# A 32-byte tile ahead of the weight pools at the right-hand end of SBUF

## The chip, the cores and the metric

The kernel runs on one core of one Trainium2 chip. The metric is the device time of one execution in microseconds, as the median of several runs. A core has five engines that the profile names: PE (TensorE, matmuls; its weight loads stand apart as PEld), DVE (VectorE), ACT (ScalarE), POOL (GpSimd) and SP (SyncE, which here issues most of the transfers). Matmuls read both operands from SBUF, the on-chip memory of 128 partitions, and write to PSUM.

## The reference

One decoder layer (DEPTH = 1) on 256 positions of width 2048, all in float32:

```python
h = rmsnorm(x, g_pre_mix)
proj = h @ w_in                      # 2048 x 15376, split into the inputs of three branches and their gates
oa = gated_head_norm(gated_deltanet(...), az, gn_a)
ob = gated_head_norm(hgrn2(...), bz, gn_b)
oc = memory_attention(cq, rmsnorm(mem, g_mem), w_kv_mem)
merged = ga * (oa @ w_br_a) + gb * (ob @ w_br_b) + gc * (oc @ w_br_c)
x = x + rmsnorm(merged @ w_out, g_post_mix)
h2 = rmsnorm(x, g_pre_mlp)
m = square(relu(h2 @ w_mlp_in)) @ w_mlp_out      # 2048 -> 8192 -> 2048
x = x + rmsnorm(m, g_post_mlp)
```

## The kernel before

Nearly all the time is matrix products of 256 positions with streamed weights. To keep float32 accuracy in the faster format fp32r, each operand is held as two parts, a high part (the value rounded to fp32r) and a low part (the rest), and each product is made as three: high by high, high by low, low by high. Activations are split once; weights are split as they arrive.

**How weights travel.** SP loads a piece of 128 partitions x 2 x 512 float32 (512 KB, 4096 bytes a partition) into a tile `w` (`load_w_raw`, line 193). `split_w` (line 203) lets ACT cast it into `wh` and DVE subtract `wh` from it into `wl`. `w`, `wh` and `wl` have four buffers each in the pool `wp` (line 84), which is placed from the right-hand end of SBUF. All other pools grow from the left.

**Which operand moves.** A matmul holds one operand (stationary, 128 columns wide, loaded by a weight load) and streams the other (moving, up to 512 columns).

- `unit` (line 216) keeps the activation stationary and moves the weights: for each of 16 or 8 rows of blocks and each half of the positions, three matmuls of 512 columns, in the order high activation with `wh`, high with `wl`, low with `wh`.
- `unit_joined` and `unit_stacked`, through `products_joined` (line 248), keep the weights stationary and move the activation's high and low part side by side: one wide matmul of 512 columns with `wh`, and one narrow one of 256 with `wl`. They make a pass of wide ones over some groups, then a pass of narrow ones, and turn the order round for the next groups.

**The stages.** First the memory's keys and values, the projections of the three branches, their inner work (which is spread between the products by generators), the gates, the three branch outputs and `w_out`; this takes `wp` throughout. The MLP follows. `first_weights` (line 1368) loads its first two groups into tiles of the general pool `gp` on the left. Then the MLP has buffers of its own:

```python
pairs = [pair_at(wx, i) for i in range(2)]            # oh0, ol0, oh1, ol1 in pool wx, on the left
raws = [at(wx, "raw0", F32)]
...
weights.close()                                       # in wide_ring: wp is given back
wy = ctx.enter_context(tc.tile_pool(name="wy", bufs=1, side="right", reuse_waits="tile"))
raws.extend(at(wy, f"raw{i}", F32) for i in range(1, 5))
raws.append(g4("raw5", (P, KG, 512)))                 # in gp, on the left
pairs.extend(pair_at(wy, i) for i in range(2, 6))
```

`wide_ring` itself uses pairs 0 and 1; after it, `operand` hands out the six pairs in turn, beginning with pair 0, and `raw` the six landing tiles. For each e of 8, `mlp_in(e)` makes 1024 columns of the hidden layer (for e = 0 the first half with `unit`, else with `unit_stacked`, `oh` and `ol` stationary, the activation `h2h` moving), and `mlp_out(e - 1)` multiplies the 1024 hidden columns of the round before with `w_mlp_out`. There `oh` and `ol` move, and the hidden activations `mh`, `ml` and their sums `sh`, `sl` are stationary. One half of the output is made with seven products in place of eight (`seven`), for which DVE also adds weight tiles. `mlp_out(e)` takes 14 such products of six matmuls each and 8 groups of `unit` with 12 matmuls each: 22 uses of a pair, 180 matmuls.

**Addresses.** Each tile of `wp`, `wy` and `wx` has 4096 bytes a partition. In this program the right-hand end is at byte 229344, which is 32 more than a multiple of 64. So the tiles of `wp` and `wy` all start 32 bytes past a multiple of 64 (96 past a multiple of 128): `w` from 180192, `wh` from 196576, `wl` from 212960, and later `raw1` to `raw4` and pairs 2 to 5 over the same bytes. On the left, `h2h` and `hh` (activations), the general pool, `wx` and the other tiles that the large products read start at multiples of 128. The left-hand pools end at 179392 at most, 800 bytes below.

The order of the instructions on each engine is set by the program and the scheduler, with waits where a buffer has to be free or filled.

Of the kernel before, what the change touches and what calls it, by code (L numbers as in the profile page):

```python
# [10 lines left out]
F32 = mybir.dt.float32  # L11
# [6 lines left out]
P = 128  # L18
# [22 lines left out]
def tile_trunk(ctx: ExitStack, tc, a):  # L41
# [38 lines left out]
    mixing = ctx.enter_context(ExitStack())  # L80
    mk = mixing.enter_context(tc.tile_pool(name="mk", bufs=1))
    lp = mixing.enter_context(tc.tile_pool(name="lp", bufs=1))
    weights = ctx.enter_context(ExitStack())
    wp = weights.enter_context(tc.tile_pool(name="wp", bufs=4, side="right"))

# [1600 lines left out]
```

## Time and profile before

| | us |
|---|---|
| median of 3 runs | 1809.43 (1809.19 to 1810.25) |
| the profiled execution | 1810.36 |
| its span, first to last instruction | 1808.6 |
| PE busy in it | 1796.2 |
| DVE busy | 1303.3 |
| ACT busy | 961.0 |
| granted TensorE clock, mean | 0.999 of full speed |

The profiled execution's time is 1.8 us above its span: that is what lies before the first and after the last instruction. A busy PE is not a PE at its peak, since a matmul's modelled duration overlaps the next one's. What one costs in a dense stream is the distance between two starts, which a window cut at two starts shows.

### The profile page before, as it was taken

The numbers are of one execution on the slowest core, as the hardware profiler recorded it, in microseconds if no ns is written. First come the engines' busy times: TensorE is split into PE (matmuls) and PEld (weight loads), VectorE is DVE, ScalarE is ACT, GpSimd is POOL, SyncE is SP. The second block draws the span as 40 slices with busy tenths as digits, with TensorE's granted clock in tenths as the row PEclk, the third lists the DMA queues.
The fourth block names the chain that finished last, engine by engine and source line by source line (L and its number), as shares of the span: only waits on it lengthen the run. The fifth ranks groups of instructions, "written<-read, shape, count | busy, mean of one in ns | idle before, by whom it ended". The sixth has DMA issues, their size and how long they took to land.

```text
span 1808.6 us, 23962 instructions
## 1 busy us (share of the span) xinstructions
PE 1796.2 (99%) x9053; PEld 1498.4 (83%) x9053; DVE 1303.3 (72%) x1764; ACT 961.0 (53%) x1217; POOL 57.9 (3%) x100
## 2 busy tenths in 40 slices
PE   9999999999999999999999999999999999999998
PEld 7888888888888888888888888888888888888886
DVE  5764768684758487797555556796979797969695
ACT  6644665454555475565444445665545454646453
POOL 0000000400030000000000000000000000000000
PEclk9999999999999999999999999999999999999999
DMA  8565545865587455555666665767767676767683
GB/s 267 203 190 163 171 155 164 221 204 155 157 211 201 137 185 161 150 177 166 179 182 186 228 214 188 236 229 233 230 224 242 218 250 205 256 202 249 205 293 138
DMA packets 188804, 362.84 MB, mean 201 GB/s; under 512 B 14456, under 2 KB 16272, under 8 KB 188304
## 3 DMA queue, kind: packets, MB, share of 16 engines
q1 hardware_dynamic: 181856, 351.32, 61.6%
q0 software_dynamic: 2304, 5.44, 1.6%
q10 hardware_dynamic: 4528, 4.54, 0.9%
q8 instruction: 71, 1.16, 0.3%
q14 instruction: 45, 0.37, 0.1%
HBM read 356.86 MB, written 4.39 MB: 200 GB/s over the span
## 4 chain that ended last, share of the span: by engine, by line
PE 82%; DVE 2%; issue 1%; DMA 0%; ACT 0%; DVEq 0%; POOLq 0%; POOL 0%
PE mm L56 78%; PE pa L56 1%; DVE ol L56 1%; PE kk L56 0%; DMA raw<-in_w_mlp_out 0%; PE bo L56 0%; PE o L56 0%; DVE relu L56 0%; PE pw L56 0%; PE pzt L56 0%; PE tr L56 0%; PE y L56 0%; PE mgT L56 0%; PE oT L56 0%; DVE raw L56 0%
## 5 line engine op out<-in xcount | busy, mean ns | idle before, releaser
L56 DVE TENSOR_TENSOR wl<-w,wh 128x1024 fp32r<-128x1024 f32 (+1 forms) x362 | 436.9, 1216 | 255.5 <-ACT wh L56 230.6
L56 ACT CAST wh<-w 128x1024 fp32r<-128x1024 f32 (+1 forms) x362 | 374.4, 1045 | 376.3 <-PE mm L56 327.1
L56 ACT CAST oh<-raw 128x1024 fp32r<-128x1024 f32 x288 | 299.6, 1051 | 285.6 <-PE mm L56 221.1
L56 DVE TENSOR_TENSOR ol<-raw,oh 128x1024 fp32r<-128x1024 f32 x288 | 342.7, 1218 | 104.4 <-ACT oh L56 70.3
L56 PE MATMUL mm<-wh,hh 128*128 128x512 f32 x1152 | 373.0, 398 | 0.0
L56 PEld LDWEIGHTS mm<-wh,hh 128*128 128x128 f32 x1152 | 216.1, 188 | 51.1
L56 PE MATMUL mm<-h2h,oh 128*128 128x512 f32 x960 | 228.9, 394 | 0.0
L56 PE MATMUL mm<-wl,hh 128*128 128x512 f32 x576 | 227.3, 395 | 0.0
L56 PEld LDWEIGHTS mm<-h2h,oh 128*128 128x128 f32 x960 | 178.5, 188 | 39.8
L56 PE MATMUL mm<-hh,wh 128*128 128x512 f32 x768 | 189.3, 397 | 0.8 <-ACT z L56 0.7
L56 PEld LDWEIGHTS mm<-hh,wh 128*128 128x128 f32 x768 | 141.0, 188 | 32.1 <-ACT z L56 0.9
L56 PE MATMUL mm<-ol,mh 128*128 128x512 f32 x372 | 146.8, 395 | 0.2
L56 PE MATMUL mm<-oh,mh 128*128 128x512 f32 x372 | 146.2, 393 | 0.0
L56 PE MATMUL mm<-oh,ml 128*128 128x512 f32 x372 | 146.1, 395 | 0.0
L56 PEld LDWEIGHTS mm<-wl,hh 128*128 128x128 f32 x576 | 108.2, 188 | 24.5
L56 PEld LDWEIGHTS mm<-h2h,ol 128*128 128x128 f32 x960 | 117.8, 189 | 3.2 <-DVE ol L56 0.6
L56 PE MATMUL mm<-h2h,ol 128*128 128x256 f32 x960 | 119.0, 281 | 0.4 <-DVE ol L56 0.4
L56 PEld LDWEIGHTS mm<-hh,wl 128*128 128x128 f32 x768 | 97.8, 188 | 4.0
L56 PE MATMUL mm<-hh,wl 128*128 128x256 f32 x768 | 100.5, 281 | 0.0
L56 PEld LDWEIGHTS mm<-ol,mh 128*128 128x128 f32 x372 | 69.8, 188 | 17.8 <-DVE ol L56 1.4
L56 PEld LDWEIGHTS mm<-oh,mh 128*128 128x128 f32 x372 | 69.9, 188 | 17.5 <-DVE acc L56 1.1
L56 PEld LDWEIGHTS mm<-oh,ml 128*128 128x128 f32 x372 | 69.9, 188 | 15.9
(363 smaller groups left out, 2217.0 us busy)
## 6 DMA issues: line engine op xcount, KB each, us to landing
w<-in_w_in SPq DMA_DIRECT2D x240, 512.0 KB, 4.1
raw<-in_w_mlp_out SPq DMA_DIRECT2D x170, 512.0 KB, 4.7
raw<-in_w_mlp_in SPq DMA_DIRECT2D x118, 512.0 KB, 4.8
w<-in_w_out SPq DMA_DIRECT2D x32, 512.0 KB, 4.3
w<-in_w_kv_mem SPq DMA_DIRECT2D x30, 512.0 KB, 4.9
w<-in_w_br_c SPq DMA_DIRECT2D x16, 512.0 KB, 3.7
w<-in_w_br_a SPq DMA_DIRECT2D x16, 512.0 KB, 4.5
w<-in_w_br_b SPq DMA_DIRECT2D x16, 512.0 KB, 3.6
```

The source lines that it names most:

```text
L56: ins = op(*args, **kwargs)
```

## The change

A pool `edge` is opened on the right ahead of `wp`, and one tile of 8 float32 a partition (32 bytes) is taken from it. Nothing writes or reads the tile. The pool stays open to the end, so `wp` and later `wy` lie 32 bytes lower: their tiles start at multiples of 64 bytes (64 past a multiple of 128), `w` from 180160, `wh` from 196544, `wl` from 212928.

```diff
     mixing = ctx.enter_context(ExitStack())
     mk = mixing.enter_context(tc.tile_pool(name="mk", bufs=1))
     lp = mixing.enter_context(tc.tile_pool(name="lp", bufs=1))
+    edge = ctx.enter_context(tc.tile_pool(name="edge", bufs=1, side="right"))
+    edge.tile([P, 8], F32, tag="edge", name="edge")
     weights = ctx.enter_context(ExitStack())
     wp = weights.enter_context(tc.tile_pool(name="wp", bufs=4, side="right"))
```

## The prediction

> **What bounds the kernel now.** I read the page first, parts 1, 2, 4 and 5.
>
> ```profile
> span 1808.6 us, 23962 instructions
> PE 1796.2 (99%) x9053; PEld 1498.4 (83%) x9053; DVE 1303.3 (72%) x1764; ACT 961.0 (53%) x1217; POOL 57.9 (3%) x100
> PEclk9999999999999999999999999999999999999999
> PE 82%; DVE 2%; issue 1%; DMA 0%; ACT 0%; DVEq 0%; POOLq 0%; POOL 0%
> L56 DVE TENSOR_TENSOR wl<-w,wh 128x1024 fp32r<-128x1024 f32 (+1 forms) x362 | 436.9, 1216 | 255.5 <-ACT wh L56 230.6
> L56 ACT CAST wh<-w 128x1024 fp32r<-128x1024 f32 (+1 forms) x362 | 374.4, 1045 | 376.3 <-PE mm L56 327.1
> L56 ACT CAST oh<-raw 128x1024 fp32r<-128x1024 f32 x288 | 299.6, 1051 | 285.6 <-PE mm L56 221.1
> L56 DVE TENSOR_TENSOR ol<-raw,oh 128x1024 fp32r<-128x1024 f32 x288 | 342.7, 1218 | 104.4 <-ACT oh L56 70.3
> ```
>
> TensorE streams nearly the whole time. ACT's casts wait for TensorE to give buffers back (327.1 and 221.1 us), not the other way. A change that adds no instruction and no wait can pay only by making matmuls shorter. In the groups "wh,hh" means moving `wh`, stationary `hh`. The mean of 390 to 400 ns is a modelled latency; matmuls overlap, so I read the distance from start to start.
>
> The kernel holds its own comparison. The six operand pairs `oh`, `ol` of the MLP are used in turn: pairs 0 and 1 lie on the left, at multiples of 64 bytes; pairs 2 to 5 on the right, 32 bytes past one. Counting uses after `wide_ring` from 0, use k takes pair k mod 6. `mlp_in(0)` uses 6, each later `mlp_in` 16, each `mlp_out` 22. The last group of `mlp_out(0)` is use 43, pair 1; the second group of the first `unit` in `mlp_out(1)` is use 65, pair 5. Both have 12 matmuls of 512 columns; windows cut at their first starts give their times. (The count in brackets takes in neighbours that reach into a window.)
>
> ```profile
> core 0: us, PE busy (x), PEclk, DMA share, GB/s
> 499.95:508.35 8.40, 8.40 (x37) 1.00 0.75 207
> ...
> 1228.33:1231.09 2.76, 2.76 (x14) 1.00 0.94 298
> 1231.09:1233.81 2.72, 2.72 (x14) 1.00 0.32 118
> 1287.09:1289.89 2.80, 2.80 (x14) 1.00 0.70 203
> 1132.01:1135.66 3.65, 3.65 (x18) 1.00 1.01 348
> 1135.66:1139.41 3.75, 3.75 (x18) 1.00 1.04 379
> 1150.57:1152.49 1.92, 1.92 (x18) 1.00 0.66 172
> 1152.49:1154.36 1.87, 1.87 (x18) 1.00 0.54 148
> 1133.85:1135.66 1.81, 1.81 (x9) 1.00 0.90 306
> 1151.53:1152.49 0.96, 0.96 (x11) 1.00 0.83 254
> ```
>
> With the moving operand at a multiple of 64 (pair 1) a matmul takes 2.72/12 = 226.7 ns; 32 bytes off (pair 5) it takes 2.80/12 = 233.3 ns. Pair 0, just after pair 5, takes 2.76/12 = 230.0: it starts at the slow pace and changes over. The attention branch earlier, all of whose `wh` and `wl` lie on the right, shows the slow pace too: 8.40 us for 36, 233.3 ns.
>
> In `mlp_in` the pairs are stationary and `h2h`, on the left, moves. Sixteen wide matmuls take 3.65 us on pairs 0 and 1, 3.75 on 2 and 3; pair 1 alone, eight of them, 1.81. So 3.75/16 = 234.4 ns becomes 226.3, 8.1 less. The narrow ones (256 columns) go the other way: 0.96/8 = 120.0 ns on pair 1, 1.87/16 = 116.9 on 2 and 3. One wide and one narrow together gain 5.0.
>
> Other tiles and stages agree:
>
> ```profile
> 1107.70 0.61 PE L56 MATMUL mm<-wh,h2h 128*128 128x512 f32 x2
> 1108.15 0.39 PE L56 MATMUL mm<-wl,h2h 128*128 128x512 f32 x1
> 1108.38 0.62 PE L56 MATMUL mm<-wh,h2h 128*128 128x512 f32 x2
> ...
> 1287.09 0.39 PE L56 MATMUL mm<-oh,mh 128*128 128x512 f32 x1
> 1287.32 0.39 PE L56 MATMUL mm<-ol,mh 128*128 128x512 f32 x1
> ...
> 1289.89 0.40 PE L56 MATMUL mm<-oh,sh 128*128 128x512 f32 x1
> ```
>
> The first three rows are from `first_weights`, whose `wh` and `wl` lie on the left in another pool: three starts in 0.68 us, 226.7 ns again.
>
> **The change part by part.** `edge` is never written or read, so it adds no instruction, DMA or wait. It takes 32 bytes, and the 800 free between left and right cover it. `wp` and `wy` move down by 32 together, so which tiles overlap, and so who waits for whom, stays. What moves is the start of `w`, `wh`, `wl`, `raw1` to `raw4` and pairs 2 to 5, and I expect the pace of pair 1 for all of them.
>
> Moving operands on the right. This row counts the matmuls that read `wh`; of these and of as many slots of `wl`, the counts below take the moving ones.
>
> ```profile
> 0.00:1122.60 1122.60, 853.83 (x2880) 1.00 0.62 186
> ...
> L56 PE MATMUL mm<-hh,wh 128*128 128x512 f32 x768 | 189.3, 397 | 0.8 <-ACT z L56 0.7
> L56 PE MATMUL mm<-memT,wh 128*128 128x512 f32 x128 | 31.7, 399 | 0.0
> L56 PE MATMUL mm<-oh,mh 128*128 128x512 f32 x372 | 146.2, 393 | 0.0
> L56 PE MATMUL mm<-oh,sh 128*128 128x512 f32 x112 | 44.6, 398 | 0.0
> L56 PE MATMUL mm<-h2h,oh 128*128 128x512 f32 x960 | 228.9, 394 | 0.0
> ```
>
> - 2880 less the 768 + 128 where `wh` is stationary leaves 1984 with `wh` moving; each product uses `wh` twice and `wl` once, so 992 more: 2976. (24 of them, of `first_weights`, lie on the left; 0.2 us.)
> - In the MLP three products of (372 + 112) each, 1452, of which 4 pairs in 6 are on the right: 968.
> - 3944 x 6.67 ns = 26.3 us.
>
> Stationary operands on the right: 896 pairs of a wide and a narrow matmul, and 4/6 of 960 = 640. 1536 x 5.0 ns = 7.7 us.
>
> The change-over after pair 5 goes: 242 moving uses of pair 0 at (2.76 - 2.72)/12 = 3.3 ns, 0.8 us, and 160 wide ones at (1.84 - 1.81)/8 = 3.8 ns, 0.6 us (1.84 is pair 0's part of the 3.65). Together 35.4 us.
>
> The other engines. The casts `wh<-w`, all on the right, take 1045 ns, those of `oh`, a third on the left, 1051; the subtractions 1216 and 1218. I count nothing for a start there; a per cent of ACT's or DVE's time lies under TensorE except at one place. Transfers into left and right can't be told apart either: the two tables of `raw`, a third of it on the left, land as `w` does.
>
> ```profile
> w<-in_w_in SPq DMA_DIRECT2D x240, 512.0 KB, 4.1
> raw<-in_w_mlp_out SPq DMA_DIRECT2D x170, 512.0 KB, 4.7
> raw<-in_w_mlp_in SPq DMA_DIRECT2D x118, 512.0 KB, 4.8
> ...
> 1278.72:1320.73 42.01, 42.01 (x181) 33.60 (x180) 40.81 (x46) 26.14 (x27) 0.00 (x0) 1.00 0.76 251
> 1365.60:1407.80 42.20, 42.15 (x182) 33.57 (x181) 41.05 (x46) 26.04 (x28) 0.00 (x0) 1.00 0.72 239
> 1539.90:1581.80 41.90, 41.90 (x181) 33.72 (x180) 41.06 (x45) 25.96 (x27) 0.00 (x0) 1.00 0.77 254
> ```
>
> What is late next is in the last three rows, `mlp_out` of three rounds (PE, weight loads, DVE, ACT, POOL). 180 matmuls at 226.7 ns would be 40.8 us, and DVE is busy 40.8 to 41.1 us there. DVE enters such a stretch up to five pairs ahead, since in `mlp_in` it has slack, so I expect it to give back about 0.3 us in each of seven stretches, 2.0 us; the ends are 0 and all that `mlp_out` gains, 968 x 6.67 ns + 0.8 = 7.3 us.
>
> 35.4 - 2.0 = 33.4 us off. The profiled execution took 1810.36 us (its span 1808.6 and 1.8 around it), 0.9 more than the median of the runs, 1809.43. Taken off the median: **1776 us**.
>
> [...]
>
> **The rivals.**
>
> 1. *The start isn't the cause, or 64 isn't the step.* Every pair that is slow lies at the right-hand end, every fast one at a multiple of 128 on the left; after the change the right-hand tiles are 64 past a multiple of 128. So the cause could be the place, or a step of 128, and nothing moves: 1809.4 us. Against: the extra is 6.7 ns, and a column costs (226.3 - 120.0)/256 = 0.415 ns, so it is 16 columns, 64 bytes, one piece of 64 more to fetch. One more piece of 128 would be 13.3 ns. And a stationary operand on the right slows the wide matmul, but quickens the narrow one, which a slow place wouldn't. For: no wide operand 64 past a multiple of 128 is in this trace. Chance 0.12.
> 2. *DVE becomes the bound of `mlp_out`* and takes all 7.3 us there: 1809.4 - 35.4 + 7.3 = 1781 us. For: 41 of 42 us busy. Against: the slack in `mlp_in` and six pairs. It lies in the forecast's range; chance 0.10.
> 3. *Slower: TensorE's granted clock gives.* A stream denser by 3% (6.7 of 233.3 ns) could be answered with a lower clock. Each 0.01 of clock costs some 17.8 us of 1776; the gain is gone at a clock of 0.981, and at 0.97 the time is 1831. Against: the windows on pair 1 and of `first_weights`' stage have 1.00, and the page has 9 in every slice. For: no fast stretch in the trace is longer than a few us. Chance 0.03. [...]
>
> **How the numbers follow.** The forecast, with rival 2 inside, holds 0.85. Its own range: 1771 with nothing given back and 3 us more from stalls that shrink with the pace; 1788 if the stationary side gains nothing (7.7 and 0.6 us) and DVE takes half of `mlp_out`'s 7.3 instead of 2.0 (1.7 more), with 2 us for rounding of the windows. Rival 1 holds 0.12, rival 3 0.03. The range given, 1771 to 1790, leaves these out. Faster by over 0.2%, which is about what a measurement of this kernel can tell from no change: 0.85; within it 0.11; slower 0.04, as a change with no effect can still measure off by that much.
>
> **What would show it.** In the trace after: 12 matmuls of `wh` and `wl` in 2.72 us at any place before 1100 us, not 2.80; wide matmuls with stationary `wh` 226 ns apart and narrow ones 120, not 117; casts and subtractions at 1045 to 1051 and 1216 to 1218 ns still; seven `mlp_out` stretches of 41 to 41.3 us with DVE nearly full; the clock at 1.00. Starts still 233 ns apart in the attention branch would make the prediction wrong by rival 1; DVE as the releaser of TensorE by over 1 us a stretch, by rival 2.

## The result and the profile after

| | before | after |
|---|---|---|
| median, us | 1809.84 (1809.19 to 1810.67) | 1793.23 (1792.62 to 1794.40) |
| ratio, with its 95% interval | | 0.9909 (0.9892 to 0.9926) |
| the profiled execution, us | 1810.36 | 1793.10 |

The changed kernel is faster by 16.6 us, half of the 33.4 that were forecast, and its time lies above the range. The page of after, first the span, then the engines, the clock and the four groups of casts and subtractions:

```profile
span 1791.4 us, 23962 instructions
...
PE 1777.5 (99%) x9053; PEld 1493.9 (83%) x9053; DVE 1303.3 (73%) x1764; ACT 960.6 (54%) x1217; POOL 57.8 (3%) x100
...
PEclk9999999999999999999999999999999999999999
...
L56 DVE TENSOR_TENSOR wl<-w,wh 128x1024 fp32r<-128x1024 f32 (+1 forms) x362 | 437.0, 1217 | 245.7 <-ACT wh L56 223.5
L56 ACT CAST wh<-w 128x1024 fp32r<-128x1024 f32 (+1 forms) x362 | 374.6, 1046 | 365.5 <-PE mm L56 296.0
L56 ACT CAST oh<-raw 128x1024 fp32r<-128x1024 f32 x288 | 299.0, 1051 | 283.0 <-PE mm L56 213.0
L56 DVE TENSOR_TENSOR ol<-raw,oh 128x1024 fp32r<-128x1024 f32 x288 | 343.4, 1221 | 100.8 <-ACT oh L56 68.0
```

The instructions are the same in number, the casts and subtractions take what they took (1046 and 1051, 1217 and 1221 ns), and the clock stays in its top tenth (0.999 on the mean, as before). PE's busy time fell by 18.7 us. So the kind of effect is the one forecast: matmuls got shorter. By how much, windows cut at matmul starts show. First three of before: 36 moving matmuls on stationary `hh` (with `wh` and `wl` moving), 15 wide ones with `wh` stationary, and a stretch of 64 wide and 64 narrow ones with `wh` and `wl` stationary. Columns are as in the prediction's windows:

```profile
683.99:692.39 8.40, 8.40 (x38) 1.00 0.29 71
189.26:192.78 3.52, 3.52 (x17) 1.00 0.85 264
637.79:660.40 22.61, 22.61 (x131) 1.00 0.66 203
```

The same three kinds after the change (the last is the same stretch of the program), then 36 moving on stationary `och` (the output of the memory attention) and another 48 on it, 12 moving of pair 3 (on the right), 12 of pair 1 (on the left), and 16 wide ones with pairs 2 and 3 stationary:

```profile
678.99:687.23 8.24, 8.24 (x38) 1.00 0.53 144
540.09:543.58 3.49, 3.49 (x16) 1.00 0.57 172
630.91:653.24 22.33, 22.33 (x132) 1.00 0.68 208
...
493.69:502.08 8.39, 8.39 (x37) 1.00 0.65 176
376.47:387.46 10.99, 10.99 (x49) 1.00 0.72 166
...
1185.33:1188.08 2.75, 2.75 (x14) 1.00 0.45 130
1215.78:1218.50 2.72, 2.72 (x14) 1.00 0.42 160
1139.72:1143.46 3.74, 3.74 (x19) 1.00 0.68 188
```

On `hh` a moving matmul takes 8.24/36 = 228.9 ns. That is 4.4 less than the 233.3 of before, and not the 226.7 of pair 1 (2.72/12), which still is the pace on the left. Pair 3 agrees: 2.75/12 = 229.2. The gain isn't even: the first `och` stretch still goes at 233.1. That isn't a matter of `och`, since the other goes at 10.99/48 = 229.0, and the 12 matmuls on `hh` just ahead of the slow one take 2.80 us, 233.5 each; what sets the pace there is open. On the stationary side the wide matmuls got almost nothing: 3.74/16 = 233.8 ns against 234.4 for pairs 2 and 3, where 226.3 was expected. With `wh` and `wl` the sum of wide and narrow fell all the same, by 0.28 us for 64 pairs, 4.4 ns a pair of the 5.0 expected: here the narrow ones became shorter, where they were to become longer.

Where the time went, by stage. The first row is before, the second after: the stretch from the first instruction to the same matmul of `first_weights` in the program (5666 matmuls in each).

```profile
0.00:1120.98 1120.98, 1117.75 (x5666) 930.79 (x5667) 751.90 (x1181) 599.48 (x792) 56.78 (x98) 1.00 0.62 185
```

```profile
0.00:1106.34 1106.34, 1102.57 (x5666) 927.54 (x5667) 751.40 (x1181) 599.60 (x792) 56.72 (x98) 1.00 0.62 188
```

Of the profiled executions' 17.3 us, 14.6 came from here, where 24.3 were expected (2976 x 6.67 and 896 x 5.0 ns). The MLP gave only 2.6 us. Its first six `mlp_out` stretches hardly moved: 251.9 us together, 252.6 before. Two of them after, the second being the longest, with PE, weight loads, DVE, ACT and POOL:

```profile
1263.30:1305.30 42.00, 41.81 (x181) 33.55 (x180) 41.04 (x46) 25.91 (x27) 0.00 (x0) 1.00 0.75 250
1436.20:1479.30 43.10, 42.39 (x182) 33.44 (x181) 41.65 (x46) 25.95 (x27) 0.00 (x0) 1.00 0.70 235
```

PE is idle for 0.19 us of the one and 0.71 of the other, where the rows of before have 0.05 at most. Its table of waits (engine, what it waited for, us in total, times, longest) names DVE:

```profile
PE mm L56 <- DVE ol L56: 1.5, 4, 0.6
```

### The profile page after: what moved, and what is told of

Same layout as the page of the kernel before. It is cut to its first block, busy times and chain, and to the rows that moved or that the text cites. A ratio compares the mean times of both kernels' runs of the same rounds, so it can differ in the third digit from the quotient of the medians.

```text
span 1791.4 us, 23962 instructions
## 1 busy us (share of the span) xinstructions
PE 1777.5 (99%) x9053; PEld 1493.9 (83%) x9053; DVE 1303.3 (73%) x1764; ACT 960.6 (54%) x1217; POOL 57.8 (3%) x100
## 4 chain that ended last, share of the span: by engine, by line
PE 82%; DVE 2%; issue 1%; ACT 0%; DMA 0%; DVEq 0%; POOLq 0%; POOL 0%
PE mm L56 77%; DVE ol L56 1%; PE pa L56 1%; PE kk L56 0%; DVE relu L56 0%; PE bo L56 0%; PE o L56 0%; DMA raw<-in_w_mlp_out 0%; PE pzt L56 0%; PE pw L56 0%; PE tr L56 0%; DVE raw L56 0%; DVE ml L56 0%; PE y L56 0%; PE mgT L56 0%
## 5 line engine op out<-in xcount | busy, mean ns | idle before, releaser
L56 DVE TENSOR_TENSOR wl<-w,wh 128x1024 fp32r<-128x1024 f32 (+1 forms) x362 | 437.0, 1217 | 245.7 <-ACT wh L56 223.5
L56 ACT CAST wh<-w 128x1024 fp32r<-128x1024 f32 (+1 forms) x362 | 374.6, 1046 | 365.5 <-PE mm L56 296.0
L56 ACT CAST oh<-raw 128x1024 fp32r<-128x1024 f32 x288 | 299.0, 1051 | 283.0 <-PE mm L56 213.0
L56 DVE TENSOR_TENSOR ol<-raw,oh 128x1024 fp32r<-128x1024 f32 x288 | 343.4, 1221 | 100.8 <-ACT oh L56 68.0
L56 PE MATMUL mm<-wh,hh 128*128 128x512 f32 x1152 | 369.2, 395 | 0.0
```

Of the source, the lines that this page charges most:

```text
L56: ins = op(*args, **kwargs)
```

## The experiments

Three theories of the pace stood at the start. **A**: what counts is the moving or stationary tile's own start, at a multiple of 128 bytes instead of 64. **B**: what counts is the distance between the starts of the two operands, taken round a circle whose length was to be found. **C**: the right-hand end itself is slow in some measure. The left-hand operands of the large products start 128 past a multiple of 256. "Distance" below is the start of the moving operand less that of the stationary one, modulo 256. Where the right-hand tile moves, it was 96 before and is 64 after; where it is stationary, 160 and 192. The edits are shown against the changed kernel, and the times in this section are medians with the ratio to before.

**1. The right-hand tiles at multiples of 128 (distance 0).**

```diff
-    edge.tile([P, 8], F32, tag="edge", name="edge")
+    edge.tile([P, 24], F32, tag="edge", name="edge")
```

> The tile at the right-hand end has 96 bytes instead of 32, so the right-hand tiles start at multiples of 128, as the left-hand ones do. Theory A (the step is 128: a moving or stationary start off a multiple of 128 costs, 6.7 ns at 96 past and 2.3 at 64 past): every pair runs at pair 1's pace, 226.7 ns for a moving matmul, 226.5 and 120 ns for wide and narrow with a stationary one on the right, and the time is 1774 to 1780 us. Theory B (what counts is the distance of the two operands' starts within 128 bytes): the same, 1774 to 1780. Theory C (the right-hand end itself is slower, and 64 is the step): nothing more than the 32-byte tile gives, 1793, moving matmuls at 229 ns. If DVE then holds mlp_out up, its seven stretches stay at 41.5 to 42 us and the time is nearer 1781.

1781.44 us, ratio 0.9843 (0.9828 to 0.9857). Windows of 36 on `och`, 36 on `hh`, 15 wide and 15 narrow with `wh` and `wl` stationary, 12 on pair 2:

```profile
491.68:499.84 8.16, 8.16 (x37) 1.00 0.63 167
678.01:686.17 8.16, 8.16 (x38) 1.00 0.66 193
537.46:540.86 3.40, 3.40 (x17) 1.00 0.55 156
297.62:299.42 1.80, 1.80 (x17) 1.00 0.57 122
1175.59:1178.31 2.72, 2.72 (x14) 1.00 0.71 209
```

Every class now has the pace of pair 1: 226.7 ns moving (8.16/36, 2.72/12) and stationary (3.40/15), 120.0 narrow. That is what the forecast had expected of 32 bytes. C falls: the right-hand end is not slow. A and B both fit.

**2. 64 bytes (distance 32).** The tile of `edge` is `[P, 16]`. 

> The tile has 64 bytes: the right-hand tiles start 32 past a multiple of 128. A (step of 128, absolute): slower than at 128; between 64 past (1793) and 96 past (1809.8) or beyond, since the start is off 64 too. B (distance): 32 instead of 96 apart; a value of its own, the same as 1809.8 if only the size of the distance round the circle counts. C (step of 64): as before, 1809.8, moving matmuls at 233.3 ns.

1808.58 us, ratio 0.9989 (0.9980 to 0.9999). 36 on `hh`, and 15 wide:

```profile
667.19:675.59 8.40, 8.40 (x37) 1.00 0.82 249
544.35:547.85 3.50, 3.50 (x17) 1.00 0.58 171
```

Hardly anything is gained, 1.9 us: 233.3 ns for both kinds (8.40/36, 3.50/15), with the tiles 32 past a multiple of 128 as at 96 past.

**3. No `edge`; the left-hand tiles moved by 96 instead**, by a tile ahead of the first constant on the left. Both sides then start 96 past a multiple of 128, for each by itself a worse start under A, but at distance 0.

```diff
-    edge = ctx.enter_context(tc.tile_pool(name="edge", bufs=1, side="right"))
-    edge.tile([P, 8], F32, tag="edge", name="edge")
...
+    const("lpad", [P, 24])
```

> The kernel before with no tile on the right, but an unused tile of 96 bytes ahead of all others on the left: both sides start 96 past a multiple of 128. A (absolute starts): nothing gets faster, and pairs 0 and 1 become slow as well, 233.3 ns and more for every moving matmul; 1810 to 1825 us. B (distance): all operands are as far apart as in the first run, every pair at 226.7 ns, 1774 to 1780 us. C: as A.

1782.21 us, ratio 0.9846 (0.9830 to 0.9862). The same four kinds of window as the first four of experiment 1:

```profile
377.09:385.25 8.16, 8.16 (x37) 1.00 0.71 159
675.68:683.84 8.16, 8.16 (x37) 1.00 0.58 162
636.32:639.72 3.40, 3.40 (x16) 1.00 0.73 231
296.88:298.68 1.80, 1.80 (x17) 1.00 0.61 167
```

The right-hand tiles lie where they lay before the change, and all matmuls are fast. This decides for B: A had to leave the time where it was or make it worse, as now the left-hand pairs are off too.

**4. How long the circle is: 224 bytes (distance 128) and 352 bytes (distance 0 modulo 256, 256 modulo 512).** The tiles of `edge` are `[P, 56]` and `[P, 88]`.

> The tile has 224 bytes: the right-hand tiles start at multiples of 256, while the left-hand ones stay 128 past one. A with a step of 128: the same as the tile of 96 bytes within 2 us. A with a step of 256: faster still, moving matmuls under 226 ns. B with a circle of 256 bytes: slower than the tile of 96 bytes by over 3 us.

> The tile on the right has 352 bytes, so a right-hand operand is 256 bytes away from a left-hand one on a circle of 512. The tile of 96 bytes (distance 0) took 1781.4 us, that of 224 (distance 128) 1805.4, so what counts is the distance, on a circle larger than 128. Circle of 256: as with 96 bytes, 1779 to 1784 us, moving matmuls 226.7 ns apart. Circle of 512: not at that pace; 1793 to 1810, over 229 ns apart.

224 bytes: 1805.38 us, ratio 0.9974 (0.9964 to 0.9984), although every right-hand tile starts at a multiple of 256. On `och`, on `hh`, and wide:

```profile
378.42:386.82 8.40, 8.40 (x37) 1.00 0.57 143
572.70:581.07 8.37, 8.37 (x38) 1.00 0.66 190
644.03:647.51 3.48, 3.48 (x16) 1.00 0.75 248
```

352 bytes: 1781.74 us, ratio 0.9842 (0.9829 to 0.9856), in the same order:

```profile
490.62:498.77 8.15, 8.15 (x37) 1.00 0.64 174
677.31:685.47 8.16, 8.16 (x37) 1.00 0.66 192
514.72:518.12 3.40, 3.40 (x16) 1.00 1.06 273
```

A distance of 128 is slow and one of 256 fast, so, of the multiples of 32 tried, the circle has 256 bytes.

**5. Only `hh` and `h2h` moved.** B says that a pair of operands counts, so moving one tile must change its own partners' pace and nothing else. `hp`, the pool that holds `hh` and later `h2h`, goes 96 bytes up, and what lies behind it keeps its place modulo 256; there is no `edge`.

```diff
+    lp0 = ctx.enter_context(tc.tile_pool(name="lp0", bufs=1))
+    lp0.tile([P, 24], F32, tag="lp0", name="lp0")
...
+    lp1 = ctx.enter_context(tc.tile_pool(name="lp1", bufs=1))
+    lp1.tile([P, 104], F32, tag="lp1", name="lp1")
```

> From the kernel before: only the activations hh and h2h (pool hp) are moved by 96 bytes, with a tile of 96 bytes ahead of their pool and one of 416 behind it, so that all other left-hand tiles keep their distance of 96 to the right-hand ones, round a circle of 512. By the distance of the two operands: moving wh and wl with stationary hh go to 226.7 ns, wide matmuls of hh with wh and of h2h with the right-hand pairs to 226.7 and narrow ones to 120; h2h with pairs 0 and 1 goes the other way, 234 and 117; wh with the memory's activations and with mgh, and pairs 2 to 5 with mh, stay at 233.3, and pairs 0 and 1 with mh stay at 226.7. 1800 x 6.67 + (768 + 624 - 336) x 5.0 ns off: 1792 to 1794 us. By the right-hand end's own place or by its distance to what ACT, DVE or the transfers touch there: the same as before for all of these, 1809 to 1811.

1797.30 us, ratio 0.9930 (0.9916 to 0.9943). On `och`, on `hh`, and wide with `wh` stationary and `hh` moving:

```profile
493.50:501.90 8.40, 8.40 (x37) 1.00 0.65 178
686.06:694.22 8.16, 8.16 (x38) 1.00 0.76 216
539.02:542.42 3.40, 3.40 (x17) 1.00 0.55 155
```

The same `wh` is fast against `hh` (226.7) and slow against `och` (233.3). No transfer, cast or place on the right has moved. The time is 3 to 5 us above the expected one. From each start to the next in the two traces, the moving matmuls on `hh` and `h2h` gave 9.8 us, where 12.0 were expected, and `mlp_out`, whose operands kept their old distance, took 1.3 us more.

**6. The sign: 160 bytes (moving less stationary 192 with the tile moving, 64 with it stationary).** The tile of `edge` is `[P, 40]`. 

> The tile on the right has 160 bytes: a right-hand operand is 64 bytes behind a left-hand one on the circle, where the 32-byte tile put it 64 ahead. By the distance with its sign (moving less stationary): what the 32-byte tile gave to moving right-hand operands, 229 ns, now goes to wide matmuls with a stationary one on the right, and moving ones on the right get what those had, 233.4 ns: 1800 to 1806 us. By the size of the distance alone: as with 32 bytes, 1791 to 1795.

1801.50 us, ratio 0.9950 (0.9936 to 0.9963), inside what the signed distance gave. On `och`, on `hh`, and wide:

```profile
494.29:502.69 8.40, 8.40 (x38) 1.00 0.63 175
665.96:674.36 8.40, 8.40 (x38) 1.00 0.84 260
518.41:521.85 3.44, 3.44 (x17) 1.00 1.05 259
```

Now the sides have changed parts: the moving class has lost its gain (233.3), the stationary one has it (3.44/15 = 229.3). So a moving operand 64 ahead is in part fast, and one 64 behind is slow. All wide windows together:

| moving less stationary, modulo 256 | 512 columns, ns | seen in |
|---|---|---|
| 0 | 226.4 to 226.7 | experiments 1, 3, 4 (352), 5 |
| 64 | 228.9 and 229.3; one stretch 233.1 | after, experiment 6 |
| 32, 96, 128, 160, 192, 224 | 232 to 234.7 | before, after, experiments 2, 4 (224), 5, 6 |

These are windows. The same comes of all wide matmuls of the large products, sorted by the addresses that each program gives its operands, as the mean distance from one start to the next (distances over 300 ns, which hold a wait, left out): 227.1 to 228.6 ns at distance 0 in experiments 1, 3 and 4 (352), 229.2 to 229.9 at 64, 232.3 to 234.1 at 32, 96, 128, 160, 192 and 224.

**7. What takes the rest at distance 0.** Experiment 1 is at the pace that the forecast assumed, and still gains 29.0 us, not 35.4. Its longest `mlp_out` stretch, as shown above for after, and its row of waits:

```profile
1427.90:1470.00 42.10, 41.48 (x182) 33.47 (x181) 40.80 (x45) 25.84 (x27) 0.00 (x0) 1.00 0.72 238
```

```profile
PE mm L56 <- DVE ol L56: 2.1, 4, 0.7
```

The theory was DVE, as in the forecast's rival 2. The following kernels all have `[P, 24]`. The first leaves out the four `add_w` of `summed`, so its products are made of other weights.

> The kernel with the tile of 96 bytes, and the four additions of weight tiles per half of the sums in mlp_out left out, so their products are of other weights. If DVE is what holds mlp_out at 41.2 to 42.1 us instead of 180 x 226.7 ns = 40.8, the stretches fall to 40.8 to 41.0 and the time to 1774.5 to 1777.5. If not, they stay as they are, and the time at 1780 to 1782.

1778.02 us, ratio 0.9823 (0.9808 to 0.9838): 3.4 us below experiment 1. The first six `mlp_out` stretches take 246.4 us together instead of 249.7. In the one that was longest DVE's work falls from 40.80 to 37.67 us, and PE has no gap:

```profile
1426.70:1467.80 41.10, 41.10 (x181) 33.60 (x181) 37.67 (x43) 26.23 (x28) 0.00 (x0) 1.00 0.74 244
```

So these additions hold up some 3.4 us in all. Could that be had without leaving work out? First the four additions of `gen_sums` went to POOL (`V.tensor_tensor` becomes `G.tensor_tensor`).

> The kernel with the tile of 96 bytes, and the four additions of gen_sums (the sums of the hidden activations, 128 x 512 each) moved from DVE to POOL, which is idle in the MLP. If DVE holds mlp_out, 2.6 us less of it in a stretch gives 0.3 to 1.0 us each back: 1775 to 1779. If POOL's reads hold DVE's two-operand instructions up, nothing or a loss: 1781 to 1785.

A miss, by far: 1808.52 us, ratio 0.9990 (0.9981 to 0.9999). PE's waits, then one of the four operations on POOL (from 1160 us on) and the same one on DVE in experiment 1:

```profile
PE mm L56 <- DVE ol L56: 19.9, 10, 3.2
```

```profile
L1505 POOL TENSOR_TENSOR relu<-relu 128x512 f32<-128x512 f32 x6 | 20.9, 3480 | 333.0 <-DVE ml L56 333.0
L56 DVE TENSOR_TENSOR relu<-relu 128x512 f32<-128x512 f32 x14 | 9.6, 684 | 0.1
```

DVE's additions of weight tiles, here (from 1160 us on) and in experiment 1:

```profile
L56 DVE TENSOR_TENSOR raw<-raw,raw 128x1024 f32<-128x1024 f32 x54 | 82.7, 1531 | 14.1 <-DMA raw<-in_w_mlp_out 13.9
L56 DVE TENSOR_TENSOR raw<-raw,raw 128x1024 f32<-128x1024 f32 x56 | 68.3, 1220 | 12.9 <-DMA raw<-in_w_mlp_out 12.3
```

By its rough spans POOL takes 3.48 us for what takes DVE 0.684. DVE's own additions are longer, too, 1531 ns instead of 1220. That POOL's reads hold them up was one case of the expectation; no run takes apart what made them longer. DVE was freed of 28 additions, and PE waited 17.8 us longer for it than in experiment 1. The clock took some of the rest. Once in each of the first six `mlp_out` stretches two matmuls start over 3 us apart, and about the end of three of these waits TensorE's granted clock falls to half, for 3.4, 6.8 and 3.4 us. The first of the three:

```profile
1364.60:1368.00 3.40, 3.14 (x8) 0.50 0.85 273
```

At half the clock these 13.6 us cost 6.8, by estimate, which with the 17.8 is about what the two spans differ by, 23.9. All runs of this kernel have a mean clock of 0.992 to 0.997, those of experiment 1 0.999.

Then the same additions stayed on DVE but were queued behind `mlp_out` (`mlp_out(e - 1, prev, ops, None)`, then `bg.append(gen_sums(rs, later))`), and in another kernel `add_w(w12, w12, w11)` was moved behind `product(6, w22, d)`.

> The kernel with the tile of 96 bytes; the sums of the hidden activations (gen_sums: four additions, two casts and two subtractions) are handed to the background list after mlp_out instead of within it, so DVE does them in the following mlp_in, where it has 14 us to spare in 44. Leaving out the additions of weights took 3.4 us off (1778.0 against 1781.4), which is what DVE held up. If that is so, this takes about 4.8 us of DVE out of each stretch and gets the same without leaving anything out: 1777 to 1779.5, stretches of 41.0 to 41.2 us. If the order of DVE's work inside the stretch matters more than its sum: 1780 to 1783.

> The kernel with the tile of 96 bytes; in the second of DVE's additions of weights in each half of the sums (w12 + w11) is issued behind the first product's subtraction instead of ahead of it. In the trace of the 96-byte kernel TensorE waits about 13 us into each mlp_out stretch, at the end of the second half of the sums, where each product costs DVE 3.1 us (addition, subtraction, adding to the sum) and TensorE 1.36. If only the amount of DVE's work in that place counts, nothing changes: 1780 to 1782.5. If the first product's subtraction is what comes late: 1777 to 1779.5.

1781.20 us, ratio 0.9840 (0.9826 to 0.9853), and 1782.02 us, 0.9846 (0.9829 to 0.9862): neither differs from experiment 1. A stretch of the first:

```profile
1256.30:1298.40 42.10, 41.50 (x182) 33.49 (x181) 39.50 (x43) 24.30 (x26) 0.00 (x0) 1.00 0.78 256
```

DVE has 39.5 us of work in 42.1, and PE is held up all the same. So DVE's sum over the stretch isn't what binds, as I had it; what is left is its order, the four loads and additions that `summed` brings at once, and that was tried next. The last two kernels cut `summed(1)` in two and make its second half, `others(1)`, later in the block; the second of them leaves the seventh `mlp_out`, after which `mlp_out_last` ends the kernel, as it was.

```diff
-            ps = unit(..., post={2: lambda ps: part(1)})
+            ps = unit(..., post={2: lambda ps: part(1)} if c == 3
+                      else {1: lambda ps: summed(1), 3: lambda ps: others(1)})
```

> The kernel with the tile of 96 bytes; the second half of the sums is cut in two pieces of two products, one behind the first group of unit and one behind the third, so DVE's burst of 12.5 us beside 5.4 of TensorE becomes two of 6.2 with two groups of unit between (5.4 us of TensorE, 2.4 of DVE). If the burst is what makes TensorE wait, the stretches come to 41.0 to 41.2 us and the time to 1777 to 1779.5, as with the additions left out (1778.0). If not: 1780 to 1783.

> The kernel with the tile of 96 bytes and the second half of the sums cut in two as in the last run, except in the last mlp_out. There the cut's six early stretches came to 41.0 to 41.7 us as expected, but the last stretch took 96.5 us instead of 93.1, since landing tiles that are held between the pieces kept a load back. If DVE's burst is the whole of what it takes back from the faster matmuls, the early stretches keep their 41.0 and the last its 93.1: 1777.5 to 1779.5 us, as with the additions left out (1778.0). If the last stretch was late for another reason, 1781 to 1783.

1781.95 us, 0.9846 (0.9831 to 0.9861). The first six stretches fell to 41.0 to 41.7 us, but the end, from the seventh `mlp_out` on, took 96.46 us instead of the 93.07 of experiment 1, which is why the second kernel leaves that alone: 1781.51 us (1778.15 to 1782.48), 0.9837 (0.9824 to 0.9851). In its profiled execution, which took 1778.15, the first six stretches take 246.4 us together, as without the additions, and this one has no gap:

```profile
1255.40:1296.40 41.00, 41.00 (x182) 33.73 (x182) 39.08 (x44) 25.92 (x28) 0.00 (x0) 1.00 0.77 257
```

But its runs spread over 4.3 us and its median is that of experiment 1. Whether the burst is what DVE's 3.4 us are lost to stays open. What these runs do show is that none of the five rearrangements clearly beats experiment 1. Experiments 1, 3 and 4 (352 bytes) and the last four rearrangements, which all compute everything, lie together at 1781.2 to 1782.2 us, some 11 to 12 us below the changed kernel and 28 to 29 below before.

## Why the prediction was wrong

The direction and the mechanism of the first sentence held: no instruction added, and matmuls shorter from start to start. The size was wrong by half. Summed from each matmul's start to the next in both traces, which hold the same matmuls in the same order, the forecast's terms came to:

| us off | forecast | measured |
|---|---|---|
| moving `wh`, `wl`, ahead of the MLP | 19.8 | 10.6 |
| stationary `wh`, `wl` | 4.5 | 3.8 |
| `mlp_out`, after what DVE was to give back | 5.3 | 1.6 |
| stationary pairs in `mlp_in`, with the change-over | 3.8 | 0.9 |
| all else | 0 | 0.3 |
| together | 33.4 | 17.2 |

By its steps:

- **The step that failed** is "I expect the pace of pair 1 for all of them". It took a start at a multiple of 64 as the condition. Pairs 0 and 1 do lie at multiples of 64, but what made them fast is that they lie at distance 0, modulo 256, from `mh`, `sh` and `h2h` (experiments 3, 4 and 5). The change brought the right-hand tiles from distance 96 to 64. Experiment 3 has them at 96 past a multiple of 128 and all of them fast (226.7 ns).
- **Moving operands, 26.3 us.** They gained 4.4 ns each in the `hh` windows and 4.0 on the mean of the starts under 300 ns apart, not 6.67. That is about 15 us, so this term was mis-sized by 11; the 10.6 and 1.6 of the table are less, as they hold the longer waits.
- **Stationary operands, 7.7 us.** Their distance went from 160 to 192, and both are slow for wide matmuls: 0.7 ns less on the mean with `wh`, 0.8 with pairs 2 to 5, where 8.1 were forecast. The term still came to 4.7 us, and that was luck: the narrow ones, which were to get 3.1 ns longer, got 3.1 shorter with `wl`. With the pairs they got only 0.7 shorter.
- **The change-over, 1.4 us.** None of it went: the matmuls that move pairs 0 and 1 have a mean of 229.6 ns, 229.2 before, and the wide ones with these pairs stationary 228.7, 228.8 before.
- **The 64 bytes.** The argument against rival 1, that 6.7 ns are 16 columns, one piece of 64 bytes, was the author's estimate from two numbers of the trace and a coincidence of sizes: no run shows such a piece. The extra at distance 64 is some 2.4 ns, a third of it, which no count of whole pieces gives.
- **Rival 1** had the right warning, that the step isn't 64 and that the trace holds no tile 64 past a multiple of 128, with the wrong outcome: it expected no change at all. Its test, starts still 233 ns apart in the attention branch, came true in the very stretch that the prediction had shown (233.1), but not elsewhere on `och` (229.0) and not on `hh` (228.9). The case that came true, a part of the pace, stood in neither.
- **DVE in `mlp_out`, 2.0 us given back.** Right in kind, too low for the pace assumed: there it is 3.4 us (the kernel without the four additions against experiment 1). In the changed kernel, at the smaller gain, 2.0 us went to longer waits of the 3.6 that the moving matmuls gave in all of `mlp_out`. The stretches that were to take 41 to 41.3 us took 41.5 to 43.1.
- **Casts, subtractions, transfers and clock** stayed, as forecast: the first two at 1046 to 1051 and 1217 to 1221 ns, the loads of `w_in`, `w_mlp_out` and `w_mlp_in` at a median of 4.2, 4.7 and 4.8 us to landing (4.1, 4.7 and 4.8 before), the mean clock at 0.999. Rival 3 didn't come.

At the full pace the sum itself was nearly right: 35.4 forecast ahead of DVE, and 1778.02 us measured with DVE out of the way, 32 less than before. Most of what is still missing lies ahead of the MLP. Experiment 1's stretch to the same matmul is 1099.92 us long, 21.1 shorter than before instead of 24.3:

```profile
0.00:1099.92 1099.92, 1096.53 (x5666) 931.85 (x5667) 751.49 (x1181) 600.28 (x792) 57.56 (x98) 1.00 0.62 189
```

By the starts, 2.7 of these 3.2 us are missing with the moving matmuls and 0.5 with the stationary ones. Why was not tried.

## What to carry to other kernels

When a fast and a slow class stand side by side in one trace, list every property in which they differ before one is made the cause: here "left", "multiple of 64", "multiple of 128" and "same distance to the partner" all fitted, and moving the other side by one padding tile told them apart. The dense streams of wide fp32r matmuls here went at 226.4 to 226.7 ns where moving and stationary tiles start at the same address modulo 256 bytes a partition, and at 232 to 234.7 at six of the seven other distances; in a stream like these, place the pools for that, and look next at the engine that feeds it (here DVE, for 3.4 us). Where a wide and a narrow matmul come in equal numbers with the weights stationary, another distance was as good or better: all such pairs together gave 9.8 us in experiment 6, with the moving operand 64 ahead, and 7.0 in experiment 1, at distance 0.

## What the runs showed of the hardware

- A matmul of 512 fp32r columns took 226.4 to 226.7 ns from start to start where moving and stationary operand start at the same place modulo 256 bytes (experiments 1, 3, 4 with 352 bytes, 5), 228.9 to 233.1 where the moving one is 64 ahead (after, experiment 6), and 232 to 234.7 at the other multiples of 32 tried. The same moving `wh` took 226.7 ns on stationary `hh` and 233.3 on `och` (experiment 5). Absolute starts made no difference in these runs: 226.7 ns with both sides at multiples of 128 (experiment 1) and with both 96 past one (experiment 3).
- A narrow one (256 columns) was slowest at distance 0 in the windows shown: 1.80/15 = 120.0 ns. On the mean over all with `wl` stationary it took 120.8 ns in experiment 1, 119.4 in before (distance 160) and 116.3 in after (192). In before 15 of them took 1.78 us, 118.7, and in after 1.70, 113.3, while the wide ones beside them were slow:

```profile
120.84:122.62 1.78, 1.78 (x18) 1.00 0.77 246
```

```profile
535.01:536.71 1.70, 1.70 (x17) 1.00 0.73 249
```

- Plain float32 was slower a column than fp32r: in before, 16 matmuls of 192 columns with both operands in float32 (`pa`) take 2.46 us, 153.8 ns each or 0.80 a column, where a wide fp32r one at 233.3 ns takes 0.46:

```profile
703.12:705.58 2.46, 2.46 (x17) 1.00 0.68 193
```

- In the kernel with the additions on POOL, two matmuls start over 3 us apart six times. About the end of three of these waits TensorE's granted clock fell to 0.50, for 3.4, 6.8 and 3.4 us.
- Why the distance counts is open, and why the circle has 256 bytes was not tried.
